# Two residual layers, MLP as seven products: a new order of the weight sums, the root inside the squared ReLU, x transposed early

## The chip, the cores and the metric

The kernel runs on one core of one Trainium2 chip. The metric is device time of one execution in microseconds (us), as the median of several runs. The engines are TensorE (PE in the profile; its weight loads are PEld), VectorE (DVE), ScalarE (ACT), GpSimd (POOL) and SyncE (SP). SP and POOL each issue DMAs; a DMA that adds to what lies at its destination is issued by POOL here, a plain load by SP. Matrix products read SBUF and accumulate in PSUM, which has eight banks of 128 x 512 f32.

## The reference

x is 512 x 1024, f32, batch 1. Two layers; per layer an attention sub-layer and an MLP, each behind an RMSNorm and added to x, then a last RMSNorm. The change touches the MLP, the step to the next layer and the last norm:

```python
h = rmsnorm(x, mlp_norm[l])                      # x * rsqrt(mean(x*x) + EPS) * gain
u = jnp.square(jax.nn.relu(jnp.einsum('bsd,df->bsf', h, w_ff1[l])))   # D_FF = 4096
x = x + jnp.einsum('bsf,fd->bsd', u, w_ff2[l])
...
return rmsnorm(x, final_norm)
```

## The kernel before

x lies transposed in SBUF: 8 chunks of 128 features, each 128 x 512 (features on partitions, the 512 rows along them). A product in f32 precision is made of three matmuls on halves (helper `three`): each operand is split into a high part, written by ScalarE as a rounded copy (`whi`, `Ah`, `h_hi`), and a low part, what VectorE subtracts from the source (`wlo`, `Al`, `h_lo`). TensorE multiplies high by high, high by low and low by high.

**MLP.** The 4096 hidden features are worked off in four groups (`g`) of 1024. A group starts with eight blocks (`k`, the units "1"): h against 128 columns of the first weight, 8 chunks x 3 matmuls of 128x512 into one accumulator bank. The banks of these blocks come from five in rotation. `evict_u` takes a block out of its bank, squares it, and writes the operands for the second product; two blocks make a pair, four pairs a group. Then come seven products with the second weight (`FORMS`), the seven products of Strassen and Winograd's scheme for 2x2 blocks: the 512 rows are two halves, as are the 1024 output columns. Each of the seven multiplies a sum of activation blocks (index `SIDE` in `Ah`, `Al`) with a sum of weight blocks (the quadrants 11, 12, 21, 22 of the second weight), in two row quarters `r`, each in its own bank: 8 `three`s or 24 matmuls of 128x512. `gather` adds the banks to one of seven sums `y[form]` in SBUF (the first group copies instead, `fresh`).

**Weight sums.** No engine adds the weight quadrants: a quadrant is loaded by SP into a buffer `kept[HOME[form]][c]` (c is one of two halves of a group's hidden features), and once it has been split, POOL adds the next quadrant to the same buffer by an accumulating DMA (`grow`), for a product further on in the order. So the buffer's contents pass through a chain of products. Before the change one buffer pair runs 11, x1 (+12), x2 (+22), x4 (+21), another 21, then x3 (12 loaded anew, +22), and a third only 22. When a product's weights have been split, the hooks in `W.then` issue the next `grow` or the next group's `fetch`.

**Order.** Each engine runs its instructions in the order in which they were recorded, except where the scheduler has moved one; DMAs of POOL's queue wait in order as well. `W.next` hands out the weights of a unit (a block, or one half c of a product) and splits up to three units ahead, into four buffers for high and low parts; a split waits until TensorE has left the buffer.

**The root.** h is x times the gain without the root of the mean square. Since the squared ReLU of a positive multiple is the squared multiple, the MLP's output can be scaled afterwards: `r2`, the reciprocal of the mean square for each row, is made in the first group, and `settle` and `add_to` multiply the sums by it in the last group. The attention has its own root in another form: `rms_a` and `rms_b` make the root for each row, put it on two diagonal matrices, and spread it over the partitions with two matmuls into `rbc` (128 x 512).

**End of a layer.** In the last group the seven sums are combined into the four quadrants of the result: `join` adds on VectorE, `merge` adds by an accumulating DMA from SBUF to SBUF on POOL's queue. In layer 0 `back` transposes the result on TensorE (four 128x128 transposes per chunk), VectorE adds it to x, and `make_h` writes the next layer's h, whose first two products start at once. In the last layer x is transposed in the last group (`turned`) and added to the result; `square`, `root`, `weigh` and `store` make the last norm and send the eight 128 x 512 pieces out.

## Time and profile before

| | before |
|---|---|
| median of 3 runs | 1173.97 us (1173.69 to 1174.61) |
| profiled execution | 1170.51 us |
| span of it (first to last instruction) | 1168.7 us, granted TensorE clock 0.997 |
| q0, the queue of POOL's DMAs | 37.23 MB, 18.5% of 16 DMA engines' span |
| q1, plain DMAs | 131.88 MB, 34.6% |

A row of the grouped view reads: line, engine, operation, destination<-sources, shapes, count | busy us in all, mean ns of one | idle time of the engine ahead of them and what ended it. A row of waits: engine, destination and line that waited <- what it waited for: us in total, times, the longest. A row of one tile or line gives ns of one as least/median/greatest, then when the first and the last started. In a timeline a row is start, duration, engine, line, operation, and in brackets the idle time ahead of it with what ended it; in the chain of waits it is start, duration, engine, tile and line. DMA rows end with the median us from issue to landing.

### The profile page before, as it was taken

Reading aid. Unit: us, or ns where it says so; the run is one execution under the profiler, and the core shown is the slowest. Engines: PE = TensorE matmul, PEld = TensorE weight load, DVE = VectorE, ACT = ScalarE, POOL = GpSimd, SP = SyncE. Lnnn points to the kernel's source line nnn. Section 1 sums busy time; section 2 is a strip of 40 time slices with the busy share of each in tenths; the row PEclk is TensorE's granted clock in tenths of the full one; section 3 lists DMA queues with packets and bytes.
Section 4 is the critical chain, followed back from the end, with each engine's and each line's share of the span. In section 5 each row is a group of like instructions: output and inputs, shape, how many; then the busy total and the mean of one; then the engine's idle time right before and its main releaser. Section 6 shows DMA issues by size and latency. Waiting matters only on the chain.

```text
span 1168.7 us, 15328 instructions
## 1 busy us (share of the span) xinstructions
PE 1147.7 (98%) x5454; PEld 952.0 (81%) x5454; DVE 813.0 (70%) x1302; ACT 652.4 (56%) x1153; POOL 213.7 (18%) x282
## 2 busy tenths in 40 slices
PE   9999999999999999999899999999999999999996
PEld 6887888888888888888688878888888888888884
DVE  7888788765545756647789877877655466476568
ACT  6455666556756446455445556655666563554554
POOL 1222443130100101002012215331201010010021
PEclk9999999999999999999999999999999999999999
DMA  7555433255844936837525553432658368276185
GB/s 246 163 151 171 123 113 109 72 190 152 212 136 105 224 128 126 224 95 157 110 72 166 168 153 109 140 96 73 225 122 229 120 124 226 93 168 192 36 173 132
DMA packets 56860, 170.11 MB, mean 146 GB/s; under 512 B 7120, under 2 KB 8144, under 8 KB 56784
## 3 DMA queue, kind: packets, MB, share of 16 engines
q1 hardware_dynamic: 46416, 131.88, 34.6%
q0 software_dynamic: 10224, 37.23, 18.5%
q8 instruction: 43, 0.70, 0.2%
q14 instruction: 33, 0.27, 0.1%
q10 hardware_dynamic: 144, 0.02, 0.0%
HBM read 138.17 MB, written 2.10 MB: 120 GB/s over the span
## 4 chain that ended last, share of the span: by engine, by line
PE 86%; DVE 5%; DMA 2%; issue 2%; ACT 1%; POOL 0%; SPq 0%; POOLq 0%; DVEq 0%; ACTq 0%
PE f L282 10%; PE f L283 10%; PE f L281 10%; PE x L282 4%; PE x L281 4%; PE x L283 4%; PE wo L281 3%; PE wo L282 3%; PE wo L283 3%; DMA q<-in_w 2%; DVE wlo L117 1%; PE T0s L567 1%; PE T1s L567 1%; PE O0s L596 0%; PE O1s L596 0%
## 5 line engine op out<-in xcount | busy, mean ns | idle before, releaser
L117 DVE TENSOR_TENSOR wlo<-raw,whi 128x1024 fp32r<-128x1024 f32 (+1 forms) x130 | 154.6, 1193 | 98.0 <-ACT whi L116 97.4
L117 DVE TENSOR_TENSOR wlo<-q,whi 128x512 fp32r<-128x512 f32 x224 | 146.0, 687 | 106.2 <-ACT whi L116 105.7
L281 PE MATMUL f<-h_hi,whi 128*128 128x512 f32 x512 | 199.6, 390 | 0.0
L283 PE MATMUL f<-h_hi,wlo 128*128 128x512 f32 x512 | 199.3, 389 | 0.0
L282 PE MATMUL f<-h_lo,whi 128*128 128x512 f32 x512 | 199.2, 389 | 0.0
L116 ACT ACTIVATE whi<-q 128x512 fp32r<-128x512 f32 x224 | 129.6, 624 | 120.3 <-PE f L282 38.1
L116 ACT ACTIVATE whi<-raw 128x1024 fp32r<-128x1024 f32 (+1 forms) x130 | 131.5, 1018 | 106.7 <-PE f L282 55.4
L794 POOL DMA_DIRECT2D q<-in_w x64 | 56.0, 878 | 558.1 <-DVE wlo L117 471.9
L281 PEld LDWEIGHTS f<-h_hi,whi 128*128 128x128 f32 x512 | 96.1, 188 | 19.9
L282 PEld LDWEIGHTS f<-h_lo,whi 128*128 128x128 f32 x512 | 96.1, 188 | 19.9
L283 PEld LDWEIGHTS f<-h_hi,wlo 128*128 128x128 f32 x512 | 96.1, 188 | 19.9
L225 DVE TENSOR_TENSOR Al<-F,Ah 128x256 fp32r<-128x256 f32 (+2 forms) x96 | 74.8, 779 | 44.1 <-ACT Ah L224 44.0
L281 PE MATMUL x<-whi,Ah 128*128 128x512 f32 x256 | 100.0, 391 | 0.0
L282 PE MATMUL x<-wlo,Ah 128*128 128x512 f32 x256 | 99.8, 390 | 0.1
L283 PE MATMUL x<-whi,Al 128*128 128x512 f32 x256 | 99.7, 389 | 0.0
L224 ACT ACTIVATE Ah<-F 128x256 fp32r<-128x256 f32 (+2 forms) x96 | 67.6, 704 | 45.7 <-DVE F L830 43.7
L282 PEld LDWEIGHTS x<-wlo,Ah 128*128 128x128 f32 x256 | 48.1, 188 | 10.4 <-DVE wlo L117 0.5
L281 PEld LDWEIGHTS x<-whi,Ah 128*128 128x128 f32 x256 | 48.1, 188 | 10.0
L283 PEld LDWEIGHTS x<-whi,Al 128*128 128x128 f32 x256 | 48.1, 188 | 9.9
L821 ACT ACTIVATE F<-f 128x512 f32<-128x512 f32 x64 | 37.6, 587 | 10.9 <-DVE Al L225 5.4
L822 ACT ACTIVATE F<-F 128x512 f32<-128x512 f32 x64 | 40.3, 630 | 1.5
L228 ACT ACTIVATE h_hi<-x,g_all 128x512 fp32r<-128x512 f32 x32 | 22.6, 718 | 26.1 <-DVE x L704 13.8
(1057 smaller groups left out, 2574.1 us busy)
## 6 DMA issues: line engine op xcount, KB each, us to landing
raw<-in_w SPq DMA_DIRECT2D x126, 512.0 KB, 3.5
q<-in_w SPq DMA_DIRECT2D x64, 512.0 KB, 5.5
q<-in_w POOLq DMA_DIRECT2D x64, 512.0 KB, 6.0
x<-in_xT SPq DMA_DIRECT2D x8, 256.0 KB, 4.3
raw<-in_w SPq DMA_DIRECT2D x8, 128.0 KB, 4.2
yx<-y POOLq DMA_DIRECT2D x2, 512.0 KB, 7.8
y<-y POOLq DMA_DIRECT2D x2, 512.0 KB, 7.7
y<-yx POOLq DMA_DIRECT2D x2, 512.0 KB, 6.0
```

The lines of the kernel that those rows point to most:

```text
L116: h = nc.scalar.activation(hi[:, a:b], raw[:, a:b], AF.Copy)
L117: self.last = h, nc.vector.tensor_tensor(out=lo[:, a:b], in0=raw[:, a:b], in1=hi[:, a:b].bitcast(F32), op=ALU.subtract)
L224: nc.scalar.activation(hi, src, AF.Copy)
L225: nc.vector.tensor_tensor(out=lo, in0=src, in1=hi.bitcast(F32), op=ALU.subtract)
L228: a = nc.scalar.activation(h_hi[:, c, :], x[:, c, :], AF.Copy, scale=g)
L281: nc.tensor.matmul(pt, ah, bh, start=first, stop=False)
L282: nc.tensor.matmul(pt, ah, bl, start=False, stop=False)
L283: nc.tensor.matmul(pt, al, bh, start=False, stop=last)
L567: nc.tensor.transpose(pt[:, off : off + P], u["w"][qi][:, kb * P : (kb + 1) * P], ident)
L794: nc.gpsimd.dma_start(t, quad(g, q, c), accum_op=ALU.add)
L821: nc.scalar.activation(t, pt, AF.Relu)
L822: nc.scalar.activation(t, t, AF.Square)
```

## The change

Four parts, all in the MLP.

1. `FORMS` becomes 11, x3, x2, 22, x1, 21, x4, and `HOME` with it. The chains of weight sums are now 11, x1 (+12) in one pair of buffers; x3 (12, +22 at once when it is fetched), x2 (+11), x4 (+21) in the second; 22, then 21 (a plain load) in the third. The number of loads and of accumulating DMAs per group stays at eight each.
2. The root goes into the hidden features: `rms_a` and `rms_b` also for the MLP, with the diagonals in the buffer `F`, and `evict_u` takes the block out on VectorE, as max(block, 0) x `rbc`, in place of ScalarE's ReLU. The first group's evictions start after its third block. `r2`, `settle` and `add_to` are gone.
3. In the last layer x is transposed in the first group (`forth`, blocks 4 to 7) and copied into four of the sums, two of them with the opposite sign; these four sums then add in the first group too.
4. The last group combines its sums in a new way (five merges and three joins), places for the results change, four `back`s of layer 0 move into the products 21 and x4 and the other four stand between the next layer's first products, and the last norm's steps are reordered; one of the eight stores goes out on ScalarE's queue.

```diff
-FORMS = ("11", "21", "x1", "22", "x2", "x3", "x4")
+FORMS = ("11", "x3", "x2", "22", "x1", "21", "x4")
 SIDE = {"11": 0, "x4": 1, "21": 2, "x3": 3, "x1": 4, "x2": 5, "22": 6}
-HOME = {"11": 0, "21": 1, "x1": 0, "22": 2, "x2": 0, "x3": 1, "x4": 0}
+HOME = {"11": 0, "x1": 0, "x3": 1, "x2": 1, "x4": 1, "22": 2, "21": 2}
...
-                nc.sync.dma_start(kept[k][c], quad(g, form, c))
-
-            def grow(g, form, q, c, over=None):
+                nc.sync.dma_start(kept[k][c], quad(g, "12" if form == "x3" else form, c))
+                if form == "x3":
+                    nc.gpsimd.dma_start(kept[k][c], quad(g, "22", c), accum_op=ALU.add)
+
+            def grow(g, form, q, c):
                 t = kept[HOME[form]][c]
-                if over:
-                    nc.sync.dma_start(t, quad(g, over, c))
-                nc.gpsimd.dma_start(t, quad(g, q, c), accum_op=ALU.add)
+                if q == form:
+                    nc.sync.dma_start(t, quad(g, q, c))
+                else:
+                    nc.gpsimd.dma_start(t, quad(g, q, c), accum_op=ALU.add)
...
-                            ("11", grow, (g, "x1", "12", c)), ("x1", grow, (g, "x2", "22", c)),
-                            ("x2", grow, (g, "x4", "21", c)), ("21", grow, (g, "x3", "22", c, "12")),
-                            ("x4", fetch, (g + 1, "11", c)), ("x3", fetch, (g + 1, "21", c)),
-                            ("22", fetch, (g + 1, "22", c))):
+                            ("11", grow, (g, "x1", "12", c)), ("x3", grow, (g, "x2", "11", c)),
+                            ("x2", grow, (g, "x4", "21", c)), ("22", grow, (g, "21", "21", c)),
+                            ("x1", fetch, (g + 1, "11", c)), ("x4", fetch, (g + 1, "x3", c)),
+                            ("21", fetch, (g + 1, "22", c))):
...
-                nc.scalar.activation(t, pt, AF.Relu)
+                nc.vector.scalar_tensor_tensor(out=t, in0=pt, scalar=0.0, in1=rbc, op0=ALU.max, op1=ALU.mult)
                 nc.scalar.activation(t, t, AF.Square)
...
-            fresh = set(FORMS)
-            home = {(1, 0): "21", (1, 1): "22", (0, 0): "x4", (0, 1): "z" if last else "x1"}
+            fresh = set(FORMS) - ({"21", "22", "x1", "x4"} if last else set())
+            home = {(1, 0): "21", (1, 1): "22", (0, 0): "x4", (0, 1): "x3"}
...
+            def forth(tb, j):
                 pt = bank("t", f"xT{tb}{j}")
                 for k in range(4):
                     nc.tensor.transpose(pt[:, k * P : (k + 1) * P], x[:, 4 * j + k, tb * P : (tb + 1) * P], ident)
+                if j == 0:
+                    nc.scalar.copy(place(tb, j), pt)
+                elif tb < 2:
+                    nc.scalar.activation(y["x1"][:, tb, :], pt, AF.Copy, scale=-1.0)
+                else:
                     nc.vector.scalar_tensor_tensor(
+                        out=place(tb, j), in0=pt, scalar=-1.0, in1=y["x1"][:, tb - 2, :], op0=ALU.mult, op1=ALU.subtract)
...
+            def diagonals():
+                f = fp.tile([P, 4, S], F32R, tag="F", name=f"diag{l}")
+                parts_ = iter((f[:, 0, :], f[:, 1, :]))
+                return lambda name: next(parts_)
...
                         if (g, k, n) == (0, 0, 6):
+                            dg = rms_a(ssq, 1.0 / D, rcol, f"m{l}", nc.vector, diagonals())
+                        if (g, k, n) == (0, 2, 4):
+                            rms_b(rbc, f"m{l}", dg)
+                    waiting.append((pt, k))
+                    if g == 0 and k < 2:
+                        continue
+                    for one, i in waiting:
+                        evict_u(one, g, i, forms)
+                    waiting = []
+                    if last and g == 0:
+                        for tb in (2 * (k % 2), 2 * (k % 2) + 1) if k > 3 else ():
+                            forth(tb, 1 - k // 6)
...
+                        if tail and last and n == 3:
+                            gather("x4", to, (0,))
+                            square(0, 0)
+                            for tb in (2, 3):
                                 root(tb)
+                            weigh(2, 0)
                             root(0)
+                            for j in (1, 0):
+                                store(2, j, True)
+                        if end and not last and (form, n) in (("21", 5), ("21", 7), ("x4", 1), ("x4", 3)):
+                            h = back({"21": 4, "x4": 6}[form] + (n % 4 == 3))
...
                     if form == "11":
                         merge("x2", "11")
+                        merge("21", "11")
+                    elif form == "x3":
+                        merge("x4", "x3")
+                    elif form == "x2":
+                        merge("x3", "x2")
+                        merge("x4", "x2")
                     elif form == "22":
+                        join("22", "x2")
+                    elif form == "x1":
+                        join("x3", "x1")
+                        join("22", "x1")
+                        if last:
+                            for tb in (0, 1, 2, 3):
+                                square(tb, 1)
+                            for tb in (0, 1):
+                                weigh(tb, 1)
+                    elif form == "21" and last:
                         for tb in (2, 3):
+                            square(tb, 0)
+                        for tb in (2, 3):
+                            weigh(tb, 1)
             if last:
+                gather("x4", to, (1,))
+                store(3, 1, True)
                 square(1, 0)
                 store(0, 0, False)
+                root(1)
+                store(3, 0, False)
                 store(0, 1, True)
                 store(1, 0, False)
+                store(1, 1, True, nc.scalar)
             else:
...
+                gather("x4", to)
                 for n, c in enumerate(CAME):
+                    if n in (3, 5):
+                        for c_ in (n - 3, n - 2):
                             h = back(c_)
```

More of the change, by code (lines that the diff above doesn't have):

```diff
@@ L937, in trunk @@
                         if (g, k, n) == (0, 0, 6):
-                            ptr = bank("t", f"rs_m{l}")
-                            for j in range(4):
-                                nc.tensor.transpose(ptr[:, j * P : (j + 1) * P], ssq[:, j * P : (j + 1) * P], ident)
-                            nc.vector.tensor_reduce(
-                                out=r2, in_=ptr.rearrange("p (j f) -> p j f", j=4), axis=AX.X, op=ALU.add)
-                            nc.vector.tensor_scalar(
-                                out=r2, in0=r2, scalar1=1.0 / D, scalar2=EPS, op0=ALU.mult, op1=ALU.add)
-                            nc.vector.reciprocal(r2, r2)
-                    evict_u(pt, g, k, forms)
-                    if end and k in (2, 3):
-                        settle(k - 2, 0)
+                            dg = rms_a(ssq, 1.0 / D, rcol, f"m{l}", nc.vector, diagonals())
[6 more added lines that the diff above has]
+                        evict_u(one, g, i, forms)
+                    waiting = []
+                    if last and g == 0:
+                        for tb in (2 * (k % 2), 2 * (k % 2) + 1) if k > 3 else ():
+                            forth(tb, 1 - k // 6)
                 for f, form in enumerate(FORMS):
```

78 lines of the change are left out of this document (3 added, 75 removed).

## Prediction

> **What bounds the kernel now.** I read the summary first, then TensorE's waits, then stretches around its gaps, and last the timelines of POOL, VectorE and ScalarE there. The profiled execution took 1170.51 us, 1.81 us more than its span; the median of the three runs, 1173.97 us, lies 3.46 us above it. I make the sum against the profiled execution and carry it to the median.
>
> ```profile
> span 1168.7 us, 15328 instructions
> PE 1147.7 (98%) x5454; PEld 952.0 (81%) x5454; DVE 813.0 (70%) x1302; ACT 652.4 (56%) x1153; POOL 213.7 (18%) x282
> ```
>
> ```profile
> PE xT L863 <- DVE y L869: 3.2, 1, 3.2
> PE yT L883 <- DVE x L884: 1.9, 1, 1.9
> PE yT L883 <- DVE yx L877: 1.8, 2, 1.4
> ```
>
> ```profile
> 417.00:495.00 78.00, 78.00 (x345) 64.58 (x345) 49.59 (x74) 41.90 (x65) 6.97 (x8) 1.00 0.60 152
> 540.00:572.00 32.00, 31.86 (x141) 26.01 (x140) 22.66 (x36) 14.33 (x24) 7.02 (x8) 1.00 0.84 164
> 572.00:592.00 20.00, 16.37 (x79) 12.65 (x78) 18.55 (x28) 9.40 (x14) 0.76 (x6) 0.91 0.16 53
> ```
>
> TensorE is busy for 98% of the span, so only three things can give time: less matrix work, its few gaps, and the stretch after its last matmul. In the stretches (start and end; length; then busy time with count for PE, PEld, DVE, ACT and POOL; granted clock; DMA share) a middle group of the MLP, 417 to 495 us, has no gap at all. The border between the layers has: 0.14 us are lost from 540 to 572 us and 3.63 us from 572 to 592 us, where the clock was also only 0.91. In the waits, the longest three are transposes: of x in the last group (3.2 us) and of the result at the border (1.9 and 1.8 us).
>
> ```profile
> 581.91 1.18 PE L281 MATMUL p<-h_hi,whi 128*128 128x512 f32 x2
> ...
> 585.70 0.39 PE L281 MATMUL p<-h_hi,whi 128*128 128x512 f32 x1
> ```
>
> ```profile
> 548.06 0.39 PE L281 MATMUL x<-whi,Ah 128*128 128x512 f32 x1
> ...
> 553.50 0.39 PE L281 MATMUL 22030_5105<-whi,Ah 128*128 128x512 f32 x1
> ```
>
> One product takes 553.50 - 548.06 = 5.44 us for 24 matmuls, 0.227 us each (a record's 0.39 us overlaps its neighbours). After the border's gaps nine matmuls take 585.70 - 581.91 = 3.79 us in place of 2.04: 1.75 us go to the lower clock. The border costs 0.14 + 3.63 + 1.75 = 5.5 us.
>
> ```profile
> 1116.29 0.39 PE L281 MATMUL 11130_10135<-whi,Ah 128*128 128x512 f32 x1
> ...
> 1160.27 0.39 PE L283 MATMUL x<-whi,Al 128*128 128x512 f32 x1
> ```
>
> ```profile
> 1164.31 0.75 DVE L907 SCALAR_TENSOR_TENSOR yx<-yx,fin,cos_t 128x512 f32<-128x512 f32 x1 [0.66 <-POOL fin L895]
> ```
>
> I call the start of the last group's first product t, here 1116.29 us. The end is at t + 52.4; the last matmul ends at t + 44.4, where seven products alone would end at t + 38.1. The difference is the 3.2 us gap and six sets of x transposes (2.6 us, below). The last weighing ends at 1165.06, 3.6 us before the end of the span: that is the price of the last store.
>
> **The change, part by part.** *The root.* Each layer gains two 128x512 matmuls that spread the root over the partitions, 4 x 0.227 = 0.9 us on the path. Everything else of the root is off it: the transposes of the sums were there before, and between them and the spreading matmuls stand 14 triples of matmuls, 9.5 us, for two reductions, POOL's power, and two diagonals on VectorE. The bound is the attention's own root, which has the same steps:
>
> ```profile
> 602.87 0.53 PE rs_a L248 x4
> 607.79 0.59 ACT rbc L276
> ```
>
> ```profile
> L117 DVE TENSOR_TENSOR wlo<-raw,whi 128x1024 fp32r<-128x1024 f32 (+1 forms) x130 | 154.6, 1193 | 98.0 <-ACT whi L116 97.4
> ```
>
> 4.9 us there; a split of 1.2 us may stand ahead on VectorE, so 3 us of cover are left. The first three blocks' evictions wait for it, but five accumulators take turns and the sixth block starts only 11 us after the third has ended.
>
> *The eviction.* 64 ScalarE evictions go, 64 VectorE ones come.
>
> ```profile
> L821 ACT ACTIVATE F<-f 128x512 f32<-128x512 f32 x64 | 37.6, 587 | 10.9 <-DVE Al L225 5.4
> L425 DVE SCALAR_TENSOR_TENSOR t0s0q<-p0s0q,rbc x1: 690/690/690, 98.0 to 98.0; 128x512 f32<-128x512 f32 x1
> ```
>
> The nearest VectorE row, the same two operands and shape, takes 0.69 us: 8 x 0.69 = 5.5 us more in a group where VectorE is busy for 49.6 of 78 us, so 55. The chain from block to operands gets 0.1 us longer. Off the path; bounds 0 to 0.1 us in each of 8 groups. Where the cover goes is the next step.
>
> *The new order.* Weight sums now grow as 12+22, then +11, then +21 in one pair of buffers, and the second and third product use the first two of them. So between splitting the second product's weights and those of the third there is one product, 5.44 us, where before there were two; in between POOL must add 11 by an accumulating DMA.
>
> ```profile
> q<-in_w POOLq DMA_DIRECT2D x64, 512.0 KB, 6.0
> DMA to landing us min/median/max: 5.2/6.0/10.5
> 548.26 1.15 ACT L116 ACTIVATE whi<-q 128x512 fp32r<-128x512 f32 x2 [1.57 <-PE 21031_5023 L283]
> L117 DVE TENSOR_TENSOR wlo<-q,whi 128x512 fp32r<-128x512 f32 x224 | 146.0, 687 | 106.2 <-ACT whi L116 105.7
> ```
>
> A split starts when TensorE starts the half product three halves before its use (548.26 against 548.06 us). The first half of the second product is then split from t - 5.4; with the operands' work and the new eviction ahead of it on VectorE it is done by t - 2.1 (1.1 us from the row at 0.69 twice, 0.7 for the eviction, 1.2 for what VectorE had left). POOL issues at t - 2.0; with 6.0 us the sum is there at t + 4.0. ScalarE's order has that split ahead of the last pair's four derived operands, which the second product now needs at t + 9.5 to 10.0 (before, the third). From landing to their last split: two ScalarE and VectorE splits and a 1024-wide pair, 4.2 us, so t + 8.2, a margin of 1.8 us. The second half lands at t + 8.3 and is split by t + 10.2, needed at t + 13.6. I take 0, the side that the median row gives; below nothing is excluded, since TensorE has no gap there now. With the row's maximum of 10.5 us it is 2.7 us in each of 8 groups.
>
> *The border.* Four of eight sets of transposes move into the last two products, where they need the sums with two chained merges: x3 into x4 and then x2 into x3.
>
> ```profile
> 543.00 0.88 POOL L794 DMA_DIRECT2D q<-in_w  x1 [3.83 <-DVE wlo L117]
> 545.57 0.86 POOL L794 DMA_DIRECT2D q<-in_w  x1 [1.69 <-DMA q<-in_w]
> 546.13 1.19 POOL L854 DMA_DIRECT2D yx<-y  x1
> 548.79 0.88 POOL L794 DMA_DIRECT2D q<-in_w  x1 [1.47 <-DVE y L846]
> 551.35 0.88 POOL L854 DMA_DIRECT2D y<-y  x1 [1.68 <-issue]
> 559.57 1.34 ACT L873 ACTIVATE y<-y,fin 128x512 f32<-128x512 f32 x2 [7.43 <-DMA y<-y]
> ```
>
> The five transfers issued from 543.00 on have landed by 559.57, 16.5 us after the first issue: they run one behind the other, about 3 us each. After the change such a train is: the first half of x4's weights at t + 6.0, two merges of 11 at t + 8.5 and 9.4, x4's second half at 10.3, and x3 into x4 at 12.5. The last has landed at t + 22.5, and at up to 3 us more since two plain loads run beside it: t + 24.5. Then x2 into x3 is issued and takes 5.2 to 6 us: t + 30. VectorE has gathered x1 and is ready at t + 29.4; two joins follow:
>
> ```profile
> L851 DVE TENSOR_TENSOR yx<-yx,yx x3: 1217/1217/1218, 570.0 to 1150.2; 128x1024 f32<-128x1024 f32 x3
> ```
>
> With 1.15 us from one start to the next they end at t + 31.2 and 32.3. TensorE comes to the first moved transposes at t + 31.3, to those that need the second join at t + 31.5: it waits 0.8 us. The other four sets stand behind the next layer's products for chunks 4, 5 and 6 (18 matmuls, 4.1 us), which cover the last gather; 0.2 us for the first of them that needs a new h. So 1.0 us stays of 5.5: -4.5 us. Bounds: merges 2 us later leave 3 us; none late leaves 0.3. Whether the short wait brings the low clock back is the other open point, 1.75 us by the rows above. The Trainium skill, "TensorE: Matmul & The Clock Gate", section "Part 1: The HAM clock gate", says that an idle window of about 3.4 us brings half rate; by it 1.0 us of waiting brings none, and the sum stays at -4.5. The rows disagree with it in part (gaps of 1.8 and 1.9 us did bring it, one of 3.2 us in the last group didn't), and by the border's rows it would be -2.8.
>
> *The tail.* All eight sets of x transposes now run in the first group. Each is four:
>
> ```profile
> 1088.29 0.44 PE xT L863 x4
> ```
>
> Six of them, 2.6 us, move ahead of t; the work is the same. The last group then has no transposes and no gap: its last matmul ends at t + 38.1. But VectorE and ScalarE don't keep up:
>
> ```profile
> L889 ACT ACTIVATE spare<-y x4: 625/632/633, 1142.9 to 1154.7; 128x512 f32<-128x512 f32 x4
> L895 POOL TENSOR_TENSOR fin<-fin,mhalf x4: 549/552/569, 1155.5 to 1163.7; 128x1 f32<-128x1 f32 x4
> L905 ACT ACTIVATE y<-y,fin x4: 705/708/726, 1156.1 to 1160.9; 128x512 f32<-128x512 f32 x4
> L846 DVE TENSOR_TENSOR yx<-yx,x x44: 671/684/689, 389.8 to 1155.6; 128x512 f32<-128x512 f32 x44
> ```
>
> Joins end at t + 32.3 as above. VectorE's queue then holds two weighings behind the squares of the same tiles, the second half of x4's last low part (done at t + 34.2, needed at 34.9), two gathers, two weighings, two roots and one weighing: t + 37.7, at about 0.65 us each. Then the gather of the first x4 half to 38.4, a store to 39.1, and the root of block 0, which waits for ScalarE: two stores (0.7 us each) behind POOL's powers (0.55 each), a third, and the square, to t + 40.3. The gather of the second x4 half stands behind that root: 40.6 to 41.2, then a store to 41.9; ScalarE squares it by 42.6, root 42.85, power 43.5, weighing 44.2, and 3.6 us of store: t + 47.8. Against t + 52.4 that is -4.6, and with 2.6 us moved ahead of t, -2.0. Bounds: TensorE's end plus the same last steps (gather, square, root, power, weighing, store: 6.3 us) gives t + 44.4, 3.4 us better; merges 2 us later give 2.2 us worse.
>
> Sum: 0.9 - 4.5 + 0 - 2.0 = -5.6 us, 1164.9 us for the profiled execution, 1168.4 us for the median.
>
> **The rivals.**
> *Late sums in the last group* (end effect). The two chained merges land at t + 32 and not 30. For it: the train of transfers is full (DMA share 0.84 from 540 to 572 us). Against: the 16.5 us are measured in that full stretch, so they hold it already. Border +2.0, tail +2.2: -1.4 us, 1172.6 us.
> *Slower: x2's weights late in every group.* The accumulating DMA behind the second product's split takes longer than 7.8 us, and the derived operands behind it on ScalarE hold TensorE. Eight groups pay what is over; from 8.5 us on it eats the whole gain. For it: the maximum of 10.5 us. Against: at t - 2 no other transfer of POOL's queue is under way, unlike in the stretch that made the long ones. At 9.5 us: 1.7 x 8 = 13.6 us, +8.0 us, 1182 us.
> *The tail at TensorE's pace.* VectorE and ScalarE work off more than I give them, and the tail ends near t + 44.4: -9.0 us, 1165.0 us. For it: queues that overlap better than a sum of rows; against: the chain through root 0 is fixed.
>
> **How the numbers follow.** Forecast 0.50, late sums 0.18, x2 late 0.20, tail at TensorE's pace 0.12. About 0.2%, 2.3 us, is what a measurement of this kernel can tell from no change. Faster: the forecast, the last rival and a sixth of the late sums, 0.65; same: the rest of those, 0.15; slower: 0.20. The forecast's own range is 1166 to 1171 us. The whole reaches below to the last rival, 1164.5; above it takes in the late sums and the start of the slower case, with 8.5 to 8.7 us per transfer (+2 us, 1176.5). What is left out is most of the slower case and little below, about 0.19.
>
> **What would show it.** Right: TensorE's waits for x transposes gone, those at the border below 1.5 us in sum, granted clock near 1.00 there; last matmul some 9 to 10 us ahead of the end, not 8; no wait of TensorE for VectorE's low parts in the middle groups. Wrong: ScalarE's waits for POOL's weight transfers followed by TensorE waiting for the operands in the second product (x2 late); joins that start later than 30.5 us after the group's first product (late sums); a wait for the spread root in the third block.

## The result, and the profile after

The changed kernel takes 1168.69 us (median of 7 runs, 1167.26 to 1170.09). Against the kernel before on the same chip the ratio is 0.9959, with a 95% interval from 0.9943 to 0.9974: 4.8 us faster (the two medians themselves lie 5.3 us apart). Taken once more beside the last experiments it came to 0.9959 again (0.9946 to 0.9971). The profiled execution took 1167.42 us with a span of 1165.6 us, only 3.1 us shorter than the span before; the profiled execution before was one of that kernel's fastest (its runs went from 1170.3 to 1176.4 us). The granted clock differs too: beside the last experiments eleven executions of the kernel before had 0.995 to 0.997, 0.9961 in the mean, and six of the changed kernel 0.996 to 0.998, 0.9970. That is about 1 us of an execution, of the size by which the ratio's gain exceeds the profiles'; in which stage it lies was not traced.

First the page's summary, and its row of the new eviction:

```profile
span 1165.6 us, 15319 instructions
PE 1147.2 (98%) x5458; PEld 951.7 (82%) x5458; DVE 856.9 (74%) x1369; ACT 608.9 (52%) x1076; POOL 218.9 (19%) x287
...
L824 DVE SCALAR_TENSOR_TENSOR F<-f,rbc 128x512 f32<-128x512 f32 x64 | 43.6, 688 | 63.7 <-PE f L283 56.2
```

VectorE has 44 us more work and ScalarE 44 us less; TensorE's own work is the same within 0.5 us. TensorE's waits (line, what it waited for, us in total, times, longest) and the stretches of the prediction show where that shift is felt and where not:

```profile
PE yT L875 <- DVE y L854: 0.7, 1, 0.7
PE rs_m L248 <- POOL ssq L238: 0.7, 1, 0.7
...
PE yT L875 <- issue: 0.3, 1, 0.3
```

```profile
417.00:495.00 78.00, 78.00 (x346) 64.59 (x345) 54.44 (x82) 36.44 (x55) 6.97 (x8) 1.00 0.58 148
540.00:572.00 32.00, 30.99 (x139) 25.23 (x138) 26.09 (x39) 13.76 (x23) 7.02 (x8) 1.00 0.82 166
572.00:592.00 20.00, 20.00 (x100) 15.75 (x99) 15.62 (x24) 8.68 (x13) 0.76 (x6) 1.00 0.18 56
```

A middle group still has no gap, with VectorE at 54.4 of 78 us. The 3.2 us wait for x in the last group is gone. At the border 1.0 us is lost (0.7 + 0.3, both inside the last products) where it was 3.8 us, and the granted clock is 1.00 from 572 to 592 us where it was 0.91. One wait is new: the root's transposes of layer 1 stood 0.7 us for POOL's sum of squares.

Four rows of TensorE's timeline divide the execution: the start of the last group of layer 0 (11030) and of layer 1 (11130), and between them the transposes for the roots of layer 1's attention (rs_a) and MLP (rs_m). Before, after, and after in a second profile (span 1165.2 us):

```profile
537.18 0.39 PE L281 MATMUL 11030_4978<-whi,Ah 128*128 128x512 f32 x1
...
602.75 0.66 PE L248 MATMUL rs_a<-edge,ssq 128*128 128x128 f32 x4
...
831.28 0.60 PE L940 MATMUL rs_m<-edge,ssq 128*128 128x128 f32 x4
```

```profile
537.89 0.39 PE L281 MATMUL 11030_4986<-whi,Ah 128*128 128x512 f32 x1
...
599.33 0.66 PE L248 MATMUL rs_a<-edge,ssq 128*128 128x128 f32 x4
...
828.99 0.66 PE L248 MATMUL rs_m<-edge,ssq 128*128 128x128 f32 x4 [0.68 <-POOL ssq L238]
...
1117.16 0.39 PE L281 MATMUL 11130_10180<-whi,Ah 128*128 128x512 f32 x1
...
1155.02 0.39 PE L283 MATMUL x<-whi,Al 128*128 128x512 f32 x1
```

```profile
537.78 0.39 PE L281 MATMUL 11030_4986<-whi,Ah 128*128 128x512 f32 x1
...
599.50 0.66 PE L248 MATMUL rs_a<-edge,ssq 128*128 128x128 f32 x4
...
828.05 0.60 PE L248 MATMUL rs_m<-edge,ssq 128*128 128x128 f32 x4
...
1116.22 0.39 PE L281 MATMUL 11130_10180<-whi,Ah 128*128 128x512 f32 x1
```

| stretch, us | before | after | second profile | forecast of the difference |
|---|---|---|---|---|
| start to 11030 (root of layer 0) | 537.18 | +0.71 | +0.60 | +0.45 |
| 11030 to rs_a (border) | 65.57 | -4.13 | -3.85 | -4.5 |
| rs_a to rs_m (attention of layer 1) | 228.53 | +1.13 | +0.02 | 0 |
| rs_m to 11130 (root, x transposes) | 285.01 | +3.16 | +3.16 | +3.05 |
| 11130 to the end (tail) | 52.41 | -3.97 | -3.43 | -4.6 |
| sum | 1168.7 | -3.1 | -3.5 | -5.6 |

In the last 10 us TensorE is done (its last matmul starts at 1155.02) and VectorE's queue works off the rest. From its timeline:

```profile
1147.50 1.23 DVE L854 TENSOR_TENSOR yx<-yx,yx 128x1024 f32<-128x1024 f32 x1 [1.14 <-DMA yx<-yx]
...
1154.83 0.68 DVE L849 TENSOR_TENSOR yx<-yx,x 128x512 f32<-128x512 f32 x1
...
1157.96 0.21 DVE L886 TENSOR_SCALAR fin<-fin 128x1 f32<-128x1 f32 x1 [1.30 <-ACT spare L881]
1158.10 0.68 DVE L849 TENSOR_TENSOR yx<-yx,x 128x512 f32<-128x512 f32 x1
...
1161.07 0.75 DVE L899 SCALAR_TENSOR_TENSOR yx<-yx,fin,cos_t 128x512 f32<-128x512 f32 x1 [0.66 <-POOL fin L887]
```

With t = 1117.16 the joins start at t + 30.3, right when the chained transfer has landed; the second x4 half is gathered at t + 40.9, behind the root of block 0, and the last scaling starts at t + 43.9. In the second profile the joins start at t + 30.8 and the last scaling at t + 44.4. TensorE's last matmul ends 10.2 us ahead of the end.

### The profile page after: what moved, and what is told of

Read it like the earlier page. It is cut to its first block, busy times and chain, and to the rows that moved or that the text cites. A ratio compares the mean times of both kernels' runs of the same rounds, so it can differ in the third digit from the quotient of the medians.

```text
span 1165.6 us, 15319 instructions
## 1 busy us (share of the span) xinstructions
PE 1147.2 (98%) x5458; PEld 951.7 (82%) x5458; DVE 856.9 (74%) x1369; ACT 608.9 (52%) x1076; POOL 218.9 (19%) x287
## 4 chain that ended last, share of the span: by engine, by line
PE 77%; DVE 6%; issue 6%; DMA 4%; ACT 2%; POOL 1%; SPq 0%; POOLq 0%; DVEq 0%; ACTq 0%
PE f L282 9%; PE f L281 9%; PE f L283 9%; PE x L282 4%; PE x L283 4%; PE x L281 4%; PE wo L281 2%; PE wo L282 2%; PE wo L283 2%; DMA q<-in_w 2%; DMA yx<-yx 2%; DVE wlo L117 2%; ACT whi L116 1%; PE T0s L567 1%; PE T1s L567 1%
## 5 line engine op out<-in xcount | busy, mean ns | idle before, releaser
L117 DVE TENSOR_TENSOR wlo<-q,whi 128x512 fp32r<-128x512 f32 x224 | 146.2, 686 | 48.7 <-ACT whi L116 48.4
L824 DVE SCALAR_TENSOR_TENSOR F<-f,rbc 128x512 f32<-128x512 f32 x64 | 43.6, 688 | 63.7 <-PE f L283 56.2
```

What stands on the lines that cost most here:

```text
L117: self.last = h, nc.vector.tensor_tensor(out=lo[:, a:b], in0=raw[:, a:b], in1=hi[:, a:b].bitcast(F32), op=ALU.subtract)
L824: nc.vector.scalar_tensor_tensor(out=t, in0=pt, scalar=0.0, in1=rbc, op0=ALU.max, op1=ALU.mult)
```

## The experiments

All are changes of the changed kernel. Each ratio is to the kernel before on the same chip, with its 95% interval; the changed kernel itself has 0.9959. Line numbers of the experiments' own texts can lie some lines further down. The table gives the same stretches as above, in us (the first is a point in time, the last runs to the end of the span). Each row is one profiled execution: "to 11030" goes from 537.5 to 540.4 us in kernels that don't differ up to there, so a difference in that column, and in a sum over a whole profile, says little; the later stretches of kernels with the same code there agree to some tenths of a microsecond. In e_best the marker rs_m itself stands two triples, 1.4 us, later.

| kernel | ratio | to 11030 | border | attention | to 11130 | tail |
|---|---|---|---|---|---|---|
| changed | 0.9959 | 537.89 | 61.44 | 229.66 | 288.17 | 48.44 |
| e_border | 0.9954 (0.9940 to 0.9967) | 539.42 | 60.79 | 229.88 | 288.23 | 48.68 |
| e_column | 0.9971 (0.9960 to 0.9982) | 540.38 | 64.44 | 228.63 | 288.17 | 48.88 |
| e_join | 0.9924 (0.9910 to 0.9938) | 537.52 | 59.98 | 228.79 | 288.17 | 46.84 |
| e_tail | 0.9946 (0.9930 to 0.9961) | 537.49 | 61.41 | 228.87 | 288.18 | 47.05 |
| e_best | 0.9931 (0.9917 to 0.9945) | 540.29 | 59.96 | 231.42 | 286.79 | 46.44 |
| e_both | 0.9917 (0.9906 to 0.9929) | 538.18 | 60.22 | 228.87 | 288.17 | 45.76 |
| e_noxt | 0.9913 (0.9898 to 0.9927) | 537.95 | 61.79 | 228.68 | 284.53 | 48.45 |
| e_evict2 | 0.9990 (0.9977 to 1.0003) | 539.79 | 62.34 | 229.99 | 288.17 | 49.91 |
| e_x2three | 1.0098 (1.0082 to 1.0115) | 543.00 | 69.67 | 229.14 | 289.54 | 53.75 |

**What removed the border's gaps: e_border.** The early transposes go back behind the last product:

```diff
-                        if end and not last and (form, n) in (("21", 5), ("21", 7), ("x4", 1), ("x4", 3)):
-                            h = back({"21": 4, "x4": 6}[form] + (n % 4 == 3))
...
+                for c in CAME[:4]:
+                    back(c)
                 gather("x4", to)
```

> Layer 0's four early sets of result transposes stand behind the last product again; all else is as in the changed kernel (1168.7 us). Theory (the border's step): what the change gained there comes from the sets lying between matmuls of the last two products, which hide the way from transpose over addition and split (about 2.2 us) to the next layer's h. Behind the last product nothing covers it: 1.5 to 3 us of gap appear, and with a gap of 1.8 us or more the low clock (another 1.7 us); the 1.0 us of waiting inside the last products goes. Net +0.5 to +4 us: 1169.2 to 1172.7 us, granted clock below 1.00 near 585 us. Rival: it was the earlier sums (t + 32 us and not later) that removed the border's gaps; the place of the transposes is worth nothing: 1167.7 to 1168.7 us, clock 1.00.

Measured 0.9954, no slower than the changed kernel; the border stretch is even 0.65 us shorter. Its waits and its stretch from 575 to 592 us:

```profile
PE yT L875 <- DVE x L876: 0.5, 1, 0.5
```

```profile
575.00:592.00 17.00, 16.50 (x86) 12.86 (x85) 13.28 (x19) 6.88 (x11) 0.76 (x6) 1.00 0.17 59
```

0.5 us is all that TensorE loses. The rival was right in that placing four sets between the last products is worth nothing, so something else in the change removed the gaps. The rival names the earlier sums; VectorE's timeline of the kernel before names another candidate:

```profile
575.19 1.40 DVE L877 SCALAR_TENSOR_TENSOR yx<-x,fin,yx 128x512 f32<-128x512 f32 x2
...
577.70 1.40 DVE L877 SCALAR_TENSOR_TENSOR yx<-yx,fin,yx 128x512 f32<-128x512 f32 x2
...
581.36 0.74 DVE L877 SCALAR_TENSOR_TENSOR yx<-x,fin,yx 128x512 f32<-128x512 f32 x1
...
583.35 0.73 DVE L877 SCALAR_TENSOR_TENSOR yx<-x,fin,yx 128x512 f32<-128x512 f32 x1
```

From 575.19 to 584.1 us, around TensorE's waits, it runs six additions scaled by token, in which accumulator banks or another sum are added to the result. After the change none is scaled. Two have become the plain gathers of the last product:

```profile
579.34 0.68 DVE L849 TENSOR_TENSOR yx<-yx,x 128x512 f32<-128x512 f32 x1
...
580.60 0.68 DVE L849 TENSOR_TENSOR yx<-yx,x 128x512 f32<-128x512 f32 x1
```

The other four are gone from VectorE: in the last group it makes 14 additions of 128x512 where it made 18 (12 gathers and these six), and the two merges more that part 4 of the change has do the rest. One of the three joins, 1.2 us, has moved too, to 562.63 us, behind product 22. By these rows some 3.8 us of VectorE's work have left the place (an estimate: four additions 0.66 us from start to start, one join 1.15).

**VectorE's load put back: e_column.** e_border with six products with 1 on VectorE in the places of the scaled additions:

```diff
+                def again(tb, j):
+                    o = place(tb, j)
+                    return nc.vector.scalar_tensor_tensor(out=o, in0=o, scalar=1.0, in1=o, op0=ALU.mult, op1=ALU.max)
+                seq = [g21[1]] + [again(tb, 1) for tb in (0, 1)] + [again(tb, 0) for tb in (0, 1)]
...
                 gather("x4", to)
+                seq += [again(tb, 0) for tb in (0, 1)]
```

> e_border (1166.8 us: all result transposes behind the last product) with six more 128x512 operations of VectorE at layer 0's end, each a product with 1 (0.7 us): two on x3 and two on x4 behind the gather of product 21, two on x4 behind its last gather. They stand where the kernel before had its six additions scaled by token (0.74 us each). Theory formed after e_border: the 5.5 us of the border before came from these, which the root inside the squared ReLU makes needless, and not from the place of the transposes. Then TensorE waits again for VectorE's additions into x, 2 to 4 us in sum, and the low clock comes back if one wait is 1.8 us or longer: 1168.5 to 1171.5 us. Rival (the joins' and sums' earlier time did it): under 0.7 us more than e_border.

Measured 0.9971, 0.0017 (2.0 us) above e_border, the two intervals just overlapping; in the profiles its border stretch is 3.65 us longer. One wait, and stretches of 2 us around it (the first number behind the length is TensorE's busy time, the one behind POOL's the granted clock):

```profile
PE yT L877 <- DVE x L878: 2.0, 1, 2.0
```

```profile
580.00:582.00 2.00, 0.13 (x1) 0.13 (x2) 2.00 (x5) 0.15 (x1) 0.00 (x0) 1.00 0.21 84
582.00:584.00 2.00, 1.87 (x11) 1.25 (x12) 2.00 (x4) 1.19 (x2) 0.00 (x0) 0.86 0.00 0
584.00:586.00 2.00, 2.00 (x5) 1.56 (x6) 2.00 (x4) 1.02 (x2) 0.00 (x0) 0.50 0.00 0
586.00:588.00 2.00, 2.00 (x8) 1.55 (x7) 1.47 (x3) 0.31 (x1) 0.00 (x0) 0.79 0.04 8
```

It is the picture of the kernel before: the same wait for VectorE's additions into x, 2.0 us (1.9 before), VectorE busy in every 2 us, and then a clock of 0.50. The six products take 0.60 us from start to start, 3.6 us, about what the change took away. So VectorE's load at this place, and not the earlier sums, made the greater part of the border's 5.5 us: 3.65 us of it in the profile. Which of the additions and the join counts for how much was not tested.

**The chained transfer: e_join.**

```diff
-                    elif form == "x3":
-                        merge("x4", "x3")
                     elif form == "x2":
-                        merge("x3", "x2")
-                        merge("x4", "x2")
+                        join("x3", "x2")
+                        merge("x4", "x3")
```

> In the last group x2 is added into x3 on VectorE (1.2 us) and x3 then into x4 by one transfer, in place of x3 into x4, x2 into x3 and x2 into x4 by three. Theory: the chained transfer that lands at t + 30 us holds the joins, so the waits of 0.3 and 0.7 us at the border and 1.1 us of the tail go: 1 to 2 us faster than the changed kernel, 1166.7 to 1167.7 us; joins begin near t + 29 us. Rival: VectorE is full there, the joins start no earlier, or the split it delays stops TensorE: 1168.5 us or more.

0.9924, so 4.1 us faster than the changed kernel: more than expected. The border is 1.5 us shorter (both waits are gone, 35.00 of 35 us busy from 540 to 575) and the tail 1.6 us: in the places that the theory named, each some 0.5 us more than it said. VectorE's timeline:

```profile
1142.57 0.68 DVE L117 TENSOR_TENSOR wlo<-q,whi 128x512 fp32r<-128x512 f32 x1
1143.17 1.22 DVE L854 TENSOR_TENSOR yx<-yx,yx 128x1024 f32<-128x1024 f32 x1
```

With t = 1114.46 the joins start at t + 28.7, 1.6 us earlier, behind a split and no longer behind a transfer. In the profile another 0.9 us lies in the attention of layer 1, where the second profile of the changed kernel had no loss either; it is no part of the edit.

**The order of the last 10 us: e_tail.**

```diff
-                            gather("x4", to, (0,))
-                            square(0, 0)
-                            for tb in (2, 3):
-                                root(tb)
-                            weigh(2, 0)
-                            root(0)
+                            dv = gather("x4", to, (0,))
+                            behind(dv[0], g21[1])
+                            sq0 = square(0, 0)
+                            dv += [root(tb) for tb in (2, 3)]
+                            dv += [weigh(2, 1), weigh(3, 1), weigh(2, 0), root(0)]
...
+                            row(*dv)
+                            row(sq0, *st)
```

> Only the order of the last layer's end is changed: on VectorE the gather of x4's first half stands ahead of the roots and the weighings of blocks 2 and 3, on ScalarE the square of block 0 ahead of the stores. Theory (the tail's step): it is the queues' order, not TensorE, that sets the last 10 us; the last store starts 2 to 3 us earlier: 1165.7 to 1166.7 us, the last store's scaling near t + 41 us and not t + 43.8 us. Rival: the joins at t + 30 us or the stores' own transfers set the end: within 0.7 us of 1168.7 us.

0.9946, 0.0013 (1.5 us) below the changed kernel, the intervals overlapping, so the times alone don't show a gain. The tail is 47.05 us: 1.4 us less by the profile (1.9 by the second one), not 2 to 3 us and more than the rival's 0.7. VectorE's last scaling starts at 1157.97, t + 42.0, so by this profile the queue's order did hold it back by 1.9 us; but from there to the end it is 5.0 us and no longer 4.5, for the stores now come close together.

**Both: e_best and e_both.** e_best also moves the root's transposes of the first group by two triples.

> The joins on VectorE (e_join: 1163.8 us) and the order of the last end (e_tail) together, and the root's transposes in the MLP's first group two triples of matmuls later, so that they don't wait for POOL's last sum (0.7 us in some profiles). Theory: both parts of the tail add up, since one brings the sums earlier and the other takes the gather of x4 out of the queue behind the roots; the end then follows TensorE: last matmul at t + 38.1 us, end near t + 45.5 us and not t + 46.8: 1161.8 to 1162.8 us. Rival: the eight stores (2.1 MB at some 400 GB/s, over 5 us of transfers) already set the end: 1163.5 us or more.

0.9931, no better than e_join, so the theory missed. The move of the root was a mistake that its waits show:

```profile
PE f L282 <- DVE h_lo L229: 2.0, 2, 1.0
```

With the transposes out of the way TensorE reaches the last chunk's low part 1.0 us too early in each layer, a wait that no profile with the transposes in their old place has. The tail, 46.44 us, still had VectorE idle for 1.44 us ahead of x4's first gather. e_both leaves the root alone and fills that gap:

```diff
+                            dv = [g21[1], weigh(2, 1), weigh(3, 1)] + [root(tb) for tb in (2, 3)]
+                            dv += gather("x4", to, (0,))
+                            sq0 = square(0, 0)
+                            dv += [weigh(2, 0), root(0)]
```

> The joins on VectorE (e_join) and an order of the last end in which VectorE weighs blocks 2 and 3 and issues their roots while it waits for x4's first half (e_best's queue stood still there for 1.4 us); the root of the first group stays where the changed kernel has it. Theory: the eight stores, 2.1 MB at 410 GB/s, are one unbroken train at e_best's end, so the end follows the first stores as well as the last product: with the first scaling some 0.8 us earlier the end is at t + 45.5 to t + 46 us, and without e_best's wait for h_lo (1.0 us in each layer) the kernel is at 0.9905 to 0.992 of the one before. Rival: nothing of e_tail adds to e_join: 0.9924 or more.

0.9917 with a tail of 45.76 us, as expected; against e_join (0.9924) the intervals overlap, so that e_both is the faster of the two rests on the profiles' tails alone, 1.1 us apart. That both are faster than the changed kernel, by some 4 to 5 us, is clear of the noise. The transfers of the last stretch, 0.4 us to a number, 1150 to 1166 us:

```profile
GB/s 0 0 0 0 0 0 0 0 0 0 271 410 410 400 410 410 405 410 154 256 410 410 379 410 103 0 0 0 0 0 0 20 0 0 0 0 0 0 0 0
```

The stores run from 1154 us, where TensorE's last matmul ends (1153.7), to 1160 us, at 410 GB/s with one dip: eight pieces of 256 KB at that rate are 5.1 us. That this train sets what is left of the tail is a reading of this row; no run tests it.

**x2's weights late: e_x2twice.**

```diff
+                    for _ in range(2 if form == "x2" else 1):
                         nc.gpsimd.dma_start(t, quad(g, q, c), accum_op=ALU.add)
```

> Each half of the second sum gets block 11 added twice by two accumulating transfers, so the sums are not the reference's. In the changed kernel the first half was issued 2.2 us before and landed 3.1 us after the start of the last group's first product (5.3 us). The second transfer must wait for the first: landing about 10.6 us after the first issue. Theory (the third step and the slower rival): over 7.8 us the derived operands of the last pair, behind the split on ScalarE, come late, by about 2.4 us with the trace's own 4.1 us from landing to operands, 2.8 us by the forecast's sum, in each of 8 groups: 19 to 23 us, 1187 to 1192 us, with TensorE waiting for Ah or Al in the second product. Rival (more cover than the sum gives, for other work fills in): under 3 us, below 1172 us.

1238.8 us, ratio 1.057: 70 us, more than three times the theory. TensorE's waits, and POOL's issues in a middle group:

```profile
PE x L281 <- ACT whi L116: 51.4, 8, 8.3
```

```profile
472.60 0.86 POOL L798 DMA_DIRECT2D q<-in_w  x1 [5.28 <-DVE wlo L117]
478.32 1.77 POOL L798 DMA_DIRECT2D q<-in_w  x2 [4.86 <-DMA q<-in_w]
488.53 1.76 POOL L798 DMA_DIRECT2D q<-in_w  x2 [8.43 <-DMA q<-in_w]
```

The wait is for the split of the sum and not for the derived operands, and it falls on the second half. (In this kernel ScalarE has the first half's split behind the last pair's derived operands, where the changed kernel has it ahead of them, so the forecast's place is not tested.) A repeated addition waits until the one before it has landed, and the second half's wait in POOL's queue behind the first half's: the fourth is issued 15.9 us after the first. Waits for this split are 51.4 us of the loss. The low clock is most of the rest: TensorE's own busy time is 1168.1 us for 1147.2, 20.9 us more, at a granted clock of 0.973.

**Three transfers in place of four: e_x2three.** The condition becomes `form == "x2" and c == 0`.

> Block 11 is added twice to the first half of the second sum only, so the sums are not the reference's; three transfers stand behind each other in place of two (e_x2twice: four). Theory formed after e_x2twice: the transfers of one queue run one behind the other, 5.3 us each from the first issue at t - 2.2 us, and what comes late is the second half's split, which the third product's second half needs started by about t + 12.4 us: three land at t + 13.7 us, 1.3 us late, in each of 8 groups: 10 us more than the changed kernel, 1177 to 1182 us, waits of TensorE for whi of x2's sum near 1.3 us each. Rival (each added transfer costs its 5.3 us at once, no cover): 40 us more. Rival (the forecast's own place, the derived operands behind the first half's split): waits for Ah or Al in the second product, 2.4 us per group.

1183.5 us, ratio 1.0098, 16 us more, but not where any theory had it. The theory's pace was too slow: the third transfer landed 2.5 to 4.6 us behind the second, not 5.3. In all groups but the first the second half is there 11.4 to 13.4 us after the group's first product starts, where the changed kernel has it after 7.7. Up to 12.6 us TensorE doesn't wait for it: the middle group from 417 to 495 us is busy for 78.00 of 78 us, with the landing 12 us after its first product (461.40). At 13.3 us TensorE waits 0.5 us, and in layer 0's first group, at 16.5 us, 1.8 us, with the low clock behind it. Most of the waits lie at the ends of the layers:

```profile
PE yT L876 <- DVE yx L855: 5.1, 1, 5.1
PE x L282 <- DVE wlo L117: 5.0, 4, 4.3
PE x L281 <- ACT whi L116: 2.3, 3, 1.6
```

In the last group the extra transfers push x4's weights and the merges back: in layer 0 the chained merge is issued 32.2 us after the group's first product in place of 25.9. In this profile, the slowest of the four runs, 8.2 us of the loss are the border, 5.3 the tail and 5.1 layer 0's first groups. For x2's second half a middle group has some 5 us of cover (7.7 to 12.6); what stands behind it in POOL's queue in a last group has too little.

**What was only moved or is off the path: e_noxt and e_evict2.**

```diff
-            fresh = set(FORMS) - ({"21", "22", "x1", "x4"} if last else set())
+            fresh = set(FORMS)
...
-                    if last and g == 0:
+                    if False:
                         for tb in (2 * (k % 2), 2 * (k % 2) + 1) if k > 3 else ():
```

> Leaves out x in the last sum before the final norm: the eight sets of transposes of x in layer 1's first group and what takes them out of the accumulators. Theory (the tail's step: the sets were only moved and are still paid, TensorE having no gap there): 8 x 0.44 = 3.5 us less, 1165.2 us. Rival: in the first group they are hidden by waits that stay, under 1 us; or they cost more than their own time, for the products' operands are late behind ScalarE's and VectorE's copies: over 4.5 us.

0.9913, 5.4 us less by the ratios; their intervals are wide enough for the theory's 3.5 us as well as for the rival's 4.5. The profile decides for the theory: the stretch that holds the transposes is 3.64 us shorter (284.53 for 288.17): their own time, 3.5 us, and no more. The other 1.0 us of its shorter profile (attention 228.68) is what the second profile of the changed kernel didn't have either. What the ratio has beyond this stays open.

```diff
                 nc.vector.scalar_tensor_tensor(out=t, in0=pt, scalar=0.0, in1=rbc, op0=ALU.max, op1=ALU.mult)
+                nc.vector.scalar_tensor_tensor(out=t, in0=pt, scalar=0.0, in1=rbc, op0=ALU.max, op1=ALU.mult)
```

> Each of the 64 evictions is done twice on VectorE: 0.69 us each, 5.5 us per group, so some 60 of 78 us busy. Theory (the second step: off the path): 0 to 0.8 us in all; no wait of TensorE for operands in the middle groups. Rival: the eviction lies on the way to the second product's derived operands, and what is left of their cover is less than 0.7 us: 0.3 us or more per group, 2.5 to 6 us.

0.9990, so 3.6 us more, clear of the noise: the rival's size, but not its place. Of its waits:

```profile
PE rs_m L248 <- POOL ssq L238: 1.4, 2, 0.7
...
PE yT L876 <- DVE yx L855: 1.3, 1, 1.3
PE 11000_3150 L281 <- ACT Ah L224: 1.0, 1, 1.0
PE x L282 <- DVE wlo L117: 0.9, 1, 0.9
PE yT L876 <- DVE y L855: 0.7, 1, 0.7
```

From the root of layer 1's MLP to its last group nothing is lost (288.17 us, as without it). In layer 0 the profile has 0.8 us at the root's transposes, which e_border has too, and 1.3 us in the first group; e_column, without this edit, waits 1.1 us for operands in that group (0.6 for Ah, 0.5 for Al), so these two are not shown to be the edit's. The border is 0.9 us longer and the tail 1.5 us (0.6 and 0.9 against the second profile). There the edit's way can be seen: POOL's first transfer for x2 is issued at t - 1.4 and not t - 2.2, in a last group the merges stand behind it, and the joins start 1.4 us later (1151.99 against a first product at 1120.29, t + 31.7).

**The changed kernel again.**

> The changed kernel once more, on the chip of these runs: 0.9943 to 0.9974 of the kernel before, 1168 to 1170 us.

0.9959. Its profile, in the first table, has no wait for POOL's sum and the attention's 1.1 us are gone: that loss comes and goes between executions of the same kernel. At the border it waits 0.7 us twice.

## Why the prediction was right, and where it was not

**The time.** 1168.4 us forecast, 1168.69 measured. The sum was 2 us too large in gain for the profiled execution (-5.6 against -3.1 and -3.5), and the 3.46 us carried from profile to median was 2.2 us too large (1168.69 - 1167.42 = 1.3 us after). The two nearly cancel, so that the median was met to 0.3 us is luck; the ratio's 4.8 us is the better measure of what the change is worth, and the forecast gain of 5.6 us was near it.

**The root.** About 0.5 us in layer 1 within the 3.16, as forecast; layer 0's +0.6 to 0.7 us lie within what the first stretch differs by between executions. TensorE never waits for the spread root. That its transposes can come to wait for POOL's sum was not foreseen; the wait comes in some executions only (five of the eleven profiles with the transposes in this place), and moving them (e_best) costs more than it.

**The eviction.** 0.69 us as taken from the one row before, and VectorE at 54.4 where 55 was forecast. "Off the path, 0 to 0.1 us in each of 8 groups" holds for middle groups; at the layers' ends e_evict2 shows that one eviction more on VectorE delays the merges. What the first one costs there was not measured. The step took the middle group's cover for every group's.

**The new order.** 0 was right: no wait for weights in the middle groups. The transfers were there sooner than in the sum, the first half at t + 3.0 for t + 4.0 and the second at t + 7.7 for 8.3. Whether the 1.8 us of margin for the derived operands is right stays open, for in e_x2twice and e_x2three the split stands behind those operands. The second half was given until t + 13.6 with 1.9 us from landing to split, so t + 11.7; in e_x2three TensorE doesn't wait for it up to t + 12.6. The slower rival's price was too small: "1.7 x 8 = 13.6 us" counted the lateness of one transfer in the first half's place, but in e_x2twice the halves' transfers stand behind each other and what is late adds up in the second half (8.3 us in the group shown), with the low clock on top.

**The border.** The size was nearly right (-4.5 against -4.1 and -3.9), and so were the landing of the chained merge (t + 30; the join starts at t + 30.45 in layer 0) and the 1.0 us that stays. The mechanism was wrong, so the size was met by luck. The step said that four of eight sets of transposes move into the last two products and that this hides the way to h; e_border puts them back at no cost. What went is VectorE's load: e_column puts 3.6 us of it back, and 3.65 us of the border return, low clock included. The prediction counted the transposes and left out what the change takes off VectorE there: four of 18 additions, which two merges more now make, and a join that comes earlier. That it is these, and in which shares, follows from the rows and was not tested one by one. The 1.0 us of waiting that the step counted as what is left stands at the moved sets; e_border, without them, waits 0.5 us, and e_join, with the chained merge gone, not at all.

**The low clock.** Right: none at 1.00 us of waits in two pieces, and none at 1.3 us in two pieces in the second profile. The gap of 1.8 us that the prediction took from the rows before is two, of 1.4 and 0.3 us.

**The tail.** -2.0 forecast with 2.6 us moved ahead of t; 3.1 us of moving and root were measured in the stretch before, and -4.0 and -3.4 behind t where -4.6 stood. The chain was right in its parts: the joins held by the chained transfer (e_join: 1.6 us), the second gather behind the root of block 0 (e_tail, by its profile). Mis-sized was the working off: the second half of x4 was to be gathered at t + 40.6 and was at t + 40.9, and the end of the store came 4.5 us after the start of the last scaling, where 0.75 + 3.6 was taken.

**The rivals.** Late sums: t + 30.3 and 30.5 in the first profile and t + 30.8 twice in the second, so past the prediction's sign of 30.5 us there, but nearer to its t + 30 than to the rival's t + 32. x2 late: no. The tail at TensorE's pace (t + 44.4): no, t + 48.4; e_both, with both causes removed, reaches t + 45.8; the stores' own 5 us probably stand in the way there.

## What to carry to other kernels

When an edit moves work between engines, list what it removes on each engine at the one place that has a gap: here the border's gain was not in the transposes that the diff moves but in additions that VectorE no longer makes at that place. An experiment that undoes one part alone (e_border) and one that puts the suspected load back (e_column) tell the two apart. Cover that is measured in a middle group doesn't hold for the last one, where merges, gathers and stores stand in the same queues. A sum against one profiled execution should be given with the spread of that kernel's runs: the constant between profile and median changed by 2.2 us, nearly half of the effect.

## What the runs showed of the hardware

- A wait of 2.0 us (e_column, with transposes on both sides of it) was followed by matmuls spaced 0.43 us and more from 583.7 to 586.9 us, 3.2 us. In e_x2three 1.63 us were enough, between matmuls of 128x512:

```profile
305.58 0.50 PE L281 MATMUL x<-whi,Ah 128*128 128x512 f32 x1 [1.63 <-ACT whi L116]
```

```profile
306.62:310.03 3.41, 3.41 (x9) 2.64 (x8) 0.23 (x1) 1.03 (x3) 0.88 (x1) 0.50 0.44 61
```

- After the 8.3 us wait of e_x2twice the matmuls were slow for hardly longer, 3.5 us from 496.9 to 500.4 us. Waits of 1.0 us (e_best) and 1.3 us (e_evict2's border) brought no slow stretch, nor did one of 2.1 us in e_x2twice (up to 928.35 us) and the 3.2 us wait for x in the last group before (1.00 in every stretch of 5 us there), so the length of the gap alone doesn't decide. The Trainium skill, "TensorE: Matmul & The Clock Gate", section "Part 1: The HAM clock gate", has a window of some 3.4 us that runs freely and of which an idle one brings half rate: the length of the slow stretches agrees with it, the gaps of 1.63 and 2.0 us that sufficed do not.
- An accumulating transfer of 512 KB that stood alone in POOL's queue landed 5.1 to 5.2 us after its issue (those issued at 454.06 and 458.79 us in the changed kernel). In the train of layer 0's last group the landings came 2.5 to 5.4 us apart. Two to the same buffer cost a full landing between their issues (472.60 and 478.32 us in e_x2twice).
- The same kernel shows 0.7 us of waiting for POOL's sum and about 1 us in layer 1's attention in one execution and not in another.
